# Mixer B's keys turned by VectorE and DMA transfers instead of TensorE, in a fused two-mixer decoder layer on one Trainium2 core

## The chip, the cores and the metric

The kernel runs on one core of a Trainium2 chip. The core has a matrix engine (TensorE, PE in the profile, with its weight loads as PEld), a vector engine (VectorE, DVE), a scalar engine (ScalarE, ACT), GpSimd (POOL), a queue processor (SyncE, SP) that mostly issues transfers, and 16 DMA engines. The metric is device time in microseconds (us), lower is better.

## What is computed

One decoder layer over 512 positions of width 1024. One input projection feeds two token mixers; a gated sum of both goes through an output projection and a layer norm with the residual:

```
h = x @ w_in + b_in
q_a, kv_a, g_nsa, z_a, q_b, f_b, i_b, z_b, gm_a, gm_b = split(h)
o_a = nsa_attention(q_a, kv_a, ...) * silu(z_a)   # 8 heads of 64: compressed, selected, window branch
o_b = hgrn2(q_b, f_b, i_b, lb)                    # 4 heads of 128, chunks of 64
o_b = o_b * rsqrt(mean(o_b^2) + eps) * norm_g * silu(z_b)
y   = sigmoid(gm_a) * (o_a @ w_branch_a) + sigmoid(gm_b) * (o_b @ w_branch_b)
out = layer_norm(alpha * x + y @ w_out)
```

The part that the change touches in mixer B (`hgrn2`) is the state update. Per head, with `k = 1 - f` and `b` the running sum of `log f` in a chunk:

```
kd    = k * exp(b_last - b)
state = dl * state + einsum('bhcd,bhce->bhde', kd, v)
```

The sum runs over positions, so the matrix engine needs `kd` with positions on the partitions; it is made with the key dimension on them. It has to be turned over, for three of the four blocks of 128 positions (the state after the last block is used by nobody).

In mixer A each query tile of 128 positions has softmax probabilities for the selected and the window branch; they too are turned, and then multiplied with the values.

## The kernel before

Everything is fp32 made of two reduced-precision halves: a projection tile is 24 matrix products of 128x512, eight steps of three (high half of the weights by high and low half of x, low half of the weights by the high half). For each weight tile SP loads `wraw`, ScalarE makes the high half (`whi`, L278) and VectorE the low half (`wlo`, L281). Two buffers hold `wraw`, three each `whi` and `wlo`.

The order of the work is written out by a small scheduler in the kernel, the weave. The projection tiles follow each other in a fixed list (queries of B qb0 to qb3, values of B, kcmp, kslc, q1, v0, v1, q0, ..., then the merge gates ga0, gb0, ga1, gb1, ... ga7, gb7, then the branch tiles b0 to b6 and a0 to a6), and every six products the clock of the weave ticks. All other work is generators (`hgrn`, `soften`, `values`, `attn_sum`, `weights`) that yield a number of ticks to wait, taken from a table `D` by `wait_of(step, ...)`. A generator that uses TensorE in a visit of its own first takes a `claim`. Matrix products, transposes and DMA issues are kept in program order on their engines; each engine runs its queue in order, and an instruction that waits holds what stands behind it. TensorE's products all carry the line of one helper, L145, its transposes L149; DMA issues carry L152 (SP), L191 (ScalarE), L194 (GpSimd).

Each projection result is formed in one of two PSUM banks `pa` and evacuated; those of B's values (`proj_i`) by VectorE at L346. The other PSUM banks are pairs as well: `pss`, `pst`, `pso`.

In `hgrn(h)` step h4 turns the keys: `transpose4` runs three 128x128 transposes on TensorE into a `pst` bank, ScalarE copies the 384 columns to SBUF (L472), and four products of 128x128 form the scores of the chunk, which VectorE masks (L478). Step h5 multiplies the turned keys with the values (three products into `pu`), and VectorE adds up the states.

In mixer A, `attn_scores` makes scores for a unit (query tile 3 window, 3 selected, 2, 2, then tile 1 and tile 0 with both branches in one unit); VectorE adds the mask and takes the minimum (L742) straight from `pss`, `pst` and `pso`; `soften` takes exponentials (ScalarE, L759), the sums and gates (L767, L770), scales (L776 on VectorE, L778 on ScalarE), and turns 32x32 blocks with VectorE's transpose into `big` (L792 to L795). Then 16 transfers on SP's queue move the 32-row blocks of `big` to their places in a `turn` buffer. There are two `turn` buffers. `values(u)` then multiplies them with the values in 64-row products into two `pso` banks, in one visit per query tile, and adds the result to `asum` (L836 and L838). `attn_sum` adds the compressed branch.

At the end VectorE finishes the last row tile in three pieces (L1133), each stored as it is made.

Of the kernel before, what the change touches and what calls it, by code (L numbers as in the profile page):

```python
# [9 lines left out]
F32 = mybir.dt.float32  # L10
# [39 lines left out]
def _columns(name):  # L50

    c = np.arange(_COLS[name], _COLS[name] + 128)
    if name[0] == "q" and name[1] != "b" or name[:2] == "za":
# [15 lines left out]

D = dict(h0=6, h2=6, h3=14, h4=0, h5=7, h6=9, n0=20, n1=4, n2=4, n3=0, n4=3, c0=4, c1=5, c2=4, c3=0, r0=5, p0=2,  # L70
         p1=35, p2=1, s0=8, s2=18, s3=4, e0=4, e1=2, t0=6, t1=10, t2=6, t3=3, a4=14, a5=7, y=2, w0=2, w1=1, x0=0,
         x1=0, e2=2, e3=2, g=3, o0=0, o1=9, o2=0, v=10)
D.update({"o0.0": 6, "w0.35": 0, "y.o.3": 6, "o1.1": 3, "h2.0": 4, "y.m.6": 8, "w0.33": 5, "w1.10": 4, "y.m.0": 1,
# [24 lines left out]


def wait_of(step, *at):  # L100
    return D.get(step + "".join(".%s" % a for a in at), D[step])

# [34 lines left out]
def layer_kernel(ctx: ExitStack, tc: tile.TileContext, xT, xn, w0, wi, wf, wv, small, brow, consts,  # L137
# [13 lines left out]
    def dma(o, i):  # L151
        tc.keep_in_program_order(nc.sync.dma_start(o, i))  # L152
# [13 lines left out]
    def T2(n=512, dt=F32):  # L166
        return t2.tile([P, n], dt, name="t2", tag="t2")
# [16 lines left out]
    def PT():  # L184
        return pst.tile([P, 512], F32, name="pst", tag="pst")
# [104 lines left out]
    ident = con[:, K_ID:K_ID + 128]  # L290
# [115 lines left out]

    def transpose4(src, n=4):
        ps = PT()
        for j in range(n):
            T.transpose(ps[:, 128 * j:128 * j + 128], src[:, 128 * j:128 * j + 128], ident)  # L410
        return ps


# [15 lines left out]
    ob = [None] * 4  # L429
    klf, osq, exps, zs = {}, {}, [], {}  # L430
    ngh = cst.tile([P, 4], F32, name="ngh")
    V.tensor_scalar(ngh, sml[:, O_NG:O_NG + 4], 0.5, None, ALU.mult)

    def hgrn(h):
# [22 lines left out]
        A.activation(dlab, cm[:, 1, :, 0], AF.Exp)  # L457
        V.tensor_tensor(e2, e2, k, ALU.mult)
        yield wait_of("h3", h)
        V.tensor_tensor(e1, e1, k, ALU.mult)  # L460
# [8 lines left out]
        yield wait_of("h4", h)  # L469
        kMT = T2()  # L470
        ps = transpose4(e2, 3)
        A.copy(kMT[:, 0:384], ps[:, 0:384])  # L472
        pst_ = PS()
# [6 lines left out]
        yield wait_of("h5", h)  # L480
        while len(vi) < 4:
            yield 1
# [22 lines left out]
        A.activation(sq, o, AF.Square)  # L505
        osq[h] = o, sq

    def hgrn_norm():
# [241 lines left out]
    def soften(visit, scores):  # L750
# [29 lines left out]
        for v, ms, ts, den, parts_ in work:  # L780
# [15 lines left out]
            if ms[-1] == 3:  # L796
                yield wait_of("t3", v)
                while spent[0] < v - 1:
                    yield 1
                w = TURN()  # L800
                to = w.bitcast(F32)[:, 0:1024 * nst].rearrange("p (a x) -> p a x", a=4)
                of = blocks[0][:, 0:1024 * nst].rearrange("p (b x) -> p b x", b=4)
                for a in range(4):
                    for b in range(4):
                        row = 32 * (b ^ 2 * (units[v][1] == (1,)))
                        dma(to[row:row + 32, a], of[32 * a:32 * a + 32, b])
                turned[0] = v + 1
                probs[v] = w.bitcast(F32)[:, 0:1024 * nst].rearrange("p (a c x) -> p c a x", a=4, x=256)
                if units[v][1][-1] == 1:
                    weave.start(values(v), wait_of("t1", v))  # L810

    def values(u):
        i = units[u][0]
        yield from weave.claim(D["t2"])
        tiles = [(v, st) for v in (u - 1, u) if units[v][0] == i for st in range(len(units[v][1]) * (i + 1))]
        accs = PO(), PO()
        todo = []
# [7 lines left out]
        for at, n, half, v, st, br, j, late in sorted(todo):  # L825
            for ab in range(2):
# [3 lines left out]
                         start=n == 0, stop=n == len(tiles) - 1)  # L830
        spent[0] = u + 1
        for half in range(2):
# [47 lines left out]
    qs = []  # L880
    wish = TURN()
    for m in range(4):
# [248 lines left out]
    V.reciprocal(ss[:, 3:4], ss[:, 3:4])  # L1131
    for hf, a, b, store in ((0, 0, 512, dma), (1, 0, 256, dma_act), (1, 256, 512, dma)):
        V.scalar_tensor_tensor(xr[hf][:, a:b], xr[hf][:, a:b], ss[:, 3:4], lbn[hf][:, a:b], ALU.mult, ALU.add)  # L1133
        store(out[384:512, 512 * hf + a:512 * hf + b], xr[hf][:, a:b])
# [79 lines left out]
```

## Time and profile before

| | before |
|---|---|
| time, median of 3 runs | 408.98 us (408.97 to 409.35) |
| profiled execution | 409.05 us, of which span 407.3 us |
| TensorE busy | 399.8 us (98%), 2119 records |
| VectorE busy | 293.6 us (72%) |
| ScalarE busy | 214.6 us (53%) |
| GpSimd busy | 20.8 us (5%) |
| granted TensorE clock | 1.00 of full speed in every stretch shown below |

The span runs from the first to the last instruction of the profiled execution; its time is 1.75 us longer. Matrix products overlap in the pipeline, so one that lasts 0.39 us can follow the one before at a distance of 0.23 us; distances between starts are what counts on TensorE. Idle time on an engine costs something only where TensorE, the one that is nearly always busy, waits for it.

### The profile page before, as it was taken

What the parts mean: (1) busy time and instruction counts of PE and PEld (TensorE: products, weight loads), DVE (VectorE), ACT (ScalarE), POOL (GpSimd) and SP (SyncE); (2) the same over time, 40 slices, a digit from 0 to 9 for tenths busy, and PEclk for the clock granted to TensorE, in tenths of its full rate; (3) what the DMA queues carried; (4) which work ended last, traced back from release to release, by engine and by line L of the source; (5) the groups of instructions that cost most, each with busy time, mean ns of one, the idle gap of its engine ahead of it and who ended that gap; (6) DMA issues with size and microseconds to landing.
All of it is one profiled execution on the core that took longest, in us unless ns stands there. A gap on an engine that the chain in (4) does not pass through costs nothing.

```text
span 407.3 us, 6081 instructions
## 1 busy us (share of the span) xinstructions
PE 399.8 (98%) x2119; PEld 323.8 (80%) x2119; DVE 293.6 (72%) x672; ACT 214.6 (53%) x445; POOL 20.8 (5%) x49
## 2 busy tenths in 40 slices
PE   9999999999999999999999999999999999999993
PEld 8888888899888887778875777867867888888883
DVE  4916599778674978898999777684622969782872
ACT  3445461642224835785688496971316748457201
POOL 2000000001530000004300000000000000000000
PEclk9999999999999999999999999999999999999998
DMA  7975820152333323372273473457958650062121
GB/s 256 378 249 207 276 95 0 32 161 85 117 86 101 123 82 116 104 174 103 64 180 129 155 188 124 106 154 198 265 143 273 206 176 34 0 213 97 52 103 53
DMA packets 26670, 57.62 MB, mean 141 GB/s; under 512 B 5136, under 2 KB 7824, under 8 KB 26640
## 3 DMA queue, kind: packets, MB, share of 16 engines
q1 hardware_dynamic: 25184, 56.69, 44.8%
q8 instruction: 17, 0.28, 0.3%
q10 hardware_dynamic: 432, 0.39, 0.3%
q0 software_dynamic: 1024, 0.15, 0.2%
q14 instruction: 13, 0.11, 0.1%
HBM read 42.12 MB, written 2.10 MB: 109 GB/s over the span
## 4 chain that ended last, share of the span: by engine, by line
PE 90%; DVE 7%; issue 1%; DVEq 0%; ACT 0%; ACTq 0%
PE pa L145 60%; PE pss L145 15%; PE pso L145 11%; PE pst L145 4%; DVE big L792 2%; DVE wlo L281 1%; DVE t L742 1%; DVE t L538 1%; DVE t L544 1%; DVE t L545 0%; PE pst L149 0%; DVE t L537 0%; DVE t L927 0%; DVE big L1133 0%; DVE t L776 0%
## 5 line engine op out<-in xcount | busy, mean ns | idle before, releaser
L145 PE MATMUL pa<-t,whi 128*128 128x512 f32 x640 | 199.9, 394 | 0.0
L145 PEld LDWEIGHTS pa<-t,whi 128*128 128x128 f32 x640 | 118.2, 188 | 28.8 <-issue 4.1
L145 PE MATMUL pa<-t,wlo 128*128 128x512 f32 x320 | 124.9, 390 | 0.1
L281 DVE TENSOR_TENSOR wlo<-wraw,whi 128x1024 fp32r<-128x1024 f32 x44 | 53.5, 1217 | 35.1 <-ACT whi L278 35.1
L278 ACT CAST whi<-wraw 128x1024 fp32r<-128x1024 f32 x44 | 45.7, 1046 | 53.5 <-PE pa L145 35.5
L145 PEld LDWEIGHTS pa<-t,wlo 128*128 128x128 f32 x320 | 60.1, 188 | 13.3 <-DVE wlo L281 0.5
L759 ACT ACTIVATE t<-t,sm_mn 128x512 f32<-128x512 f32 (+3 forms) x64 | 35.2, 552 | 14.9 <-DVE sm_mn L742 14.7
L145 PE MATMUL pso<-t,t 128*128 128x512 f32 (+2 forms) x158 | 33.2, 346 | 0.0
L145 PE MATMUL pss<-t,t 128*128 128x512 f32 (+2 forms) x158 | 30.4, 324 | 0.0
L145 PEld LDWEIGHTS pso<-t,t 128*128 128x128 f32 x158 | 25.8, 195 | 4.1 <-ACT t L237 0.3
L145 PE MATMUL pa<-t,t 128*128 128x512 f32 (+1 forms) x104 | 27.2, 366 | 0.0
L145 PEld LDWEIGHTS pss<-t,t 128*128 128x128 f32 x158 | 23.9, 190 | 2.9
L792 DVE STREAM_TRANSPOSE big<-t 128x512 f32<-128x512 f32 (+3 forms) x48 | 23.5, 523 | 2.2 <-PE pss L145 2.2
L145 PEld LDWEIGHTS pa<-t,t 128*128 128x128 f32 x104 | 18.3, 188 | 3.1
L778 ACT ACTIVATE t<-t,sm_mn 128x128 f32<-128x128 f32 (+3 forms) x42 | 18.6, 512 | 2.5 <-DVE sm_mn L770 2.5
L145 PE MATMUL pa<-turn,t 128*128 128x512 f32 x64 | 19.9, 389 | 0.0
L145 PE MATMUL pss<-t,whi 128*128 128x512 f32 x64 | 19.8, 391 | 0.0
L1007 ACT ACTIVATE t<-pa,hbias 128x512 f32<-128x512 f32 x16 | 10.9, 679 | 12.0 <-PE pa L145 12.0
L205 ACT CAST t<-t 128x512 fp32r<-128x512 f32 x16 | 9.7, 619 | 13.0 <-DVE t L1025 9.5
L145 PE MATMUL pso<-turn,t 64*64 64x512 f32 (+1 forms) x160 | 16.4, 552 | 0.0
L742 DVE CUSTOM_DVE_ANT_0 t<-pss,t 128x128 f32<-128x128 f32 (+3 forms) x24 | 10.2, 476 | 7.4 <-PE pss L145 7.4
L145 PE MATMUL pst<-t,t 128*128 128x512 f32 (+2 forms) x80 | 15.1, 345 | 0.0
(203 smaller groups left out, 531.1 us busy)
## 6 DMA issues: line engine op xcount, KB each, us to landing
wraw<-in_wf_dram SPq DMA_DIRECT2D x38, 512.0 KB, 3.5
turn<-big SPq DMA_DIRECT2D x48, 128.0 KB, 3.6
wraw<-in_wbr_dram SPq DMA_DIRECT2D x8, 512.0 KB, 4.1
t<-in_wout_dram SPq DMA_DIRECT2D x16, 256.0 KB, 4.3
turn<-big SPq DMA_DIRECT2D x32, 96.0 KB, 2.2
t<-in_wi_dram SPq DMA_DIRECT2D x8, 256.0 KB, 5.1
big<-in_w_dram SPq DMA_DIRECT2D x8, 256.0 KB, 7.7
t<-t SPq DMA_DIRECT2D x32, 64.0 KB, 2.0
```

Source lines behind the costliest of these rows:

```text
L145: return tc.keep_in_program_order(nc.tensor.matmul(*a, **k))
L205: A.copy(dst_hi, src)
L278: A.copy(hi, raws[i])
L281: V.tensor_tensor(lo, raws[i], hi.bitcast(F32), ALU.subtract)
L538: V.transpose(rms[h], osq[h][1])
L544: V.tensor_tensor(o, o, rms[h], ALU.mult)
L742: V.tensor_tensor_reduce(out=p[:, c], in0=pg[ab][:, 256 * z:][:, c], in1=amask[:, 512 - n:512], op0=ALU.add, op1=ALU.min, scale=-0.125, sc ...
L759: A.activation(p, p, AF.Exp, bias=mn[:, h:h + 1], scale=-1.0, accum_out=den[:, h:h + 1])
L778: A.mul(p, p, d)
L792: V.transpose(to, of)
L1007: A.activation(gm[name], ps, AF.Tanh, bias=hbias[:, m:m + 1], scale=0.5)
```

## The change

Mixer B's keys no longer go through TensorE. VectorE turns the 32x32 blocks inside the 128x384 tile `e2` in one instruction (into `kT`), and a new generator `turn_keys` moves the blocks to their places in `kMT` by 16 transfers per head, each of 32 rows by 3 pieces of 32 elements, in turn on SP's and on GpSimd's queue. `kT` and `kMT` lie in `keyt`, the second `turn` buffer, which nobody uses at that time. Step h5 waits until all transfers of its head are issued (`keyed`), and their arrival is waited for by the products.

Every turned block of mixer A is moved by 8 transfers on SP and 8 on GpSimd instead of 16 on SP. The values of query tiles 1 and 0 are multiplied in one visit, into `pso` (tile 0) and `pst` banks (tile 1). The last row tile is stored in pieces of 512, 384 and 128 columns instead of 512, 256 and 256. The table `D` of delays has new numbers, so that many instructions stand in another place; of it a few entries are shown.

```diff
-D = dict(h0=6, h2=6, h3=14, h4=0, h5=7, h6=9, n0=20, n1=4, n2=4, n3=0, n4=3, c0=4, c1=5, c2=4, c3=0, r0=5, p0=2,
+D = dict(k0=5, k1=1, h0=6, h2=6, h3=14, h4=0, h5=7, h6=9, n0=20, n1=4, n2=4, n3=0, n4=3, c0=5, c1=5, c2=4, c3=0,
...
-    def transpose4(src, n=4):
-        ps = PT()
-        for j in range(n):
-            T.transpose(ps[:, 128 * j:128 * j + 128], src[:, 128 * j:128 * j + 128], ident)
-        return ps
...
-    klf, osq, exps, zs = {}, {}, [], {}
+    klf, osq, exps, zs, keyed = {}, {}, [], {}, set()
...
         V.tensor_tensor(e2, e2, k, ALU.mult)
+        kT, kMT = (keyt[:, 768 * h + n:768 * h + n + 384] for n in (0, 384))
+        V.transpose(kT, e2[:, 0:384])
+        weave.start(turn_keys(h, kT, kMT), wait_of("k0", h))
         yield wait_of("h3", h)
...
         yield wait_of("h4", h)
-        kMT = T2()
-        ps = transpose4(e2, 3)
-        A.copy(kMT[:, 0:384], ps[:, 0:384])
         pst_ = PS()
...
         yield wait_of("h5", h)
-        while len(vi) < 4:
+        while len(vi) < 4 or h not in keyed:
             yield 1
...
+    def turn_keys(h, src, dst):
+        of, to = (t.rearrange("p (t a x) -> p a t x", t=3, a=4) for t in (src, dst))
+        for a in range(4):
+            for b in range(4):
+                (dma, dma_pool)[b % 2](to[32 * a:32 * a + 32, b], of[32 * b:32 * b + 32, a])
+            yield wait_of("k1", h)
+        keyed.add(h)
...
-                        dma(to[row:row + 32, a], of[32 * a:32 * a + 32, b])
+                        (dma, dma_pool)[b % 2](to[row:row + 32, a], of[32 * a:32 * a + 32, b])
...
-                if units[v][1][-1] == 1:
-                    weave.start(values(v), wait_of("t1", v))
-
-    def values(u):
+                if units[v][1][-1] == 1 and units[v][0] != 1:
+                    weave.start(values(v, *((v - 1,) if units[v][0] == 0 else ())), wait_of("t1", v))
+
+    def values(*done):
+        yield from weave.claim(D["t2"])
+        for u, bank in zip(done, (PO, PT)):
+            products(u, bank(), bank())
+
+    def products(u, *accs):
         i = units[u][0]
-        yield from weave.claim(D["t2"])
...
-        accs = PO(), PO()
...
-    wish = TURN()
+    wish, keyt = TURN(), TURN().bitcast(F32)
...
-    for hf, a, b, store in ((0, 0, 512, dma), (1, 0, 256, dma_act), (1, 256, 512, dma)):
+    for hf, a, b, store in ((0, 0, 512, dma), (1, 0, 384, dma_act), (1, 384, 512, dma)):
```

TensorE, where heads' keys were turned, in the tile q1 (names: `pst<-con,t` is a transpose, `pss<-t,t` the chunk's scores, `pa<-t,whi` and `pa<-t,wlo` the projection). Before:

```order
L145 MATMUL pa<-t_246,whi 128x512
L145 MATMUL pa<-t_247,whi 128x512
L145 MATMUL pa<-t_246,wlo 128x512
L149 MATMUL pst<-con,t_631 128x128 x3
L145 MATMUL pss<-t_661,t_630 128x128 x4
L149 MATMUL pst<-con,t_692 128x128 x3
L145 MATMUL pss<-t_763,t_691 128x128 x4
L145 MATMUL pa<-t_270,whi 128x512
```

And now, in the same tile:

```order
L146 MATMUL pa<-t_197,wlo 128x512
L146 MATMUL pss<-t_653,t_631 128x128 x4
L146 MATMUL pa<-t_222,whi 128x512
L146 MATMUL pa<-t_223,whi 128x512
L146 MATMUL pa<-t_222,wlo 128x512
L146 MATMUL pa<-t_246,whi 128x512
L146 MATMUL pa<-t_247,whi 128x512
L146 MATMUL pa<-t_246,wlo 128x512
L146 MATMUL pss<-t_794,t_705 128x128 x4
L146 MATMUL pa<-t_270,whi 128x512
```

The two sets of scores stand apart and have no transposes ahead of them; of the transposes of `L149` one is left in the whole program (another use, in mixer A).

SP's queue at that time (`wraw` is a weight tile's load, here of v0, v1 and q0; `64x256 x4` moves the rows of the compressed keys, which VectorE adds up right ahead of v1's `wlo`; `32x3x32` are the transfers of the turned keys). Before:

```order
L152 DMA big<-in_w_dram 128x512 x8
L152 DMA wraw<-in_wf_dram 128x1024 x2
L152 DMA t_824<-t_822 64x256 x4
L152 DMA t_855<-in_wv_dram 128x280
L152 DMA t_861<-in_wv_dram 128x280
L152 DMA wraw<-in_wf_dram 128x1024
```

And now:

```order
L153 DMA big<-in_w_dram 128x512 x8
L153 DMA turn<-turn 32x3x32 x10
L153 DMA wraw<-in_wf_dram 128x1024
L153 DMA turn<-turn 32x3x32 x6
L153 DMA wraw<-in_wf_dram 128x1024
L153 DMA turn<-turn 32x3x32 x4
L153 DMA t_875<-t_873 64x256 x4
L153 DMA turn<-turn 32x3x32 x2
L153 DMA t_904<-in_wv_dram 128x280
L153 DMA t_910<-in_wv_dram 128x280
L153 DMA wraw<-in_wf_dram 128x1024
```

Ten transfers stand ahead of the first of these loads, 16 ahead of the second, 20 ahead of the compressed keys' rows.

VectorE around the low half of gb1's weights (`wlo`; `big<-t 128x3x4x32` are transposes of probabilities, `ngh` marks the output of mixer B). Before:

```order
L545 SCALAR_TENSOR_TENSOR t_1481<-t_1481,ngh,t_1585 128x512
L792 STREAM_TRANSPOSE big<-t_1883 128x3x4x32
L792 STREAM_TRANSPOSE big<-t_1885 128x3x4x32
L792 STREAM_TRANSPOSE big<-t_2059 128x3x4x32
L792 STREAM_TRANSPOSE big<-t_2061 128x3x4x32
L792 STREAM_TRANSPOSE big<-t_2063 128x3x4x32
L792 STREAM_TRANSPOSE big<-t_2065 128x3x4x32
L792 STREAM_TRANSPOSE big<-t_2067 128x3x4x32
L792 STREAM_TRANSPOSE big<-t_2069 128x3x4x32
L281 TENSOR_TENSOR wlo<-wraw,whi 128x1024 x2
```

And now:

```order
L541 STREAM_TRANSPOSE t_2313<-t_1521 128x512
L773 TENSOR_TENSOR sm_mn<-sm_mn,gat 128x2 x2
L770 RECIPROCAL sm_mn<-sm_mn 128x2
L547 TENSOR_TENSOR t_1507<-t_1507,t_2286 128x512
L773 TENSOR_TENSOR sm_mn<-sm_mn,gat 128x2
L547 TENSOR_TENSOR t_1328<-t_1328,t_2298 128x512
L282 TENSOR_TENSOR wlo<-wraw,whi 128x1024
L548 SCALAR_TENSOR_TENSOR t_1507<-t_1507,ngh,t_1732 128x512
L548 SCALAR_TENSOR_TENSOR t_1328<-t_1328,ngh,t_2098 128x512
L547 TENSOR_TENSOR t_1520<-t_1520,t_2313 128x512
L795 STREAM_TRANSPOSE big<-t_2104 128x3x4x32
```

Gb1's `wlo` has moved out from behind the eight transposes, and from behind mixer B's last three products with `ngh` (the two instructions of `L281` at the end of the piece before are those of gb1 and ga2).

## Rows read from the trace of the kernel before

**Rows 1.** The page, parts 1 and 2: busy time of each engine, share of the span and instructions; the TensorE clock granted in each of 40 slices of the span, in tenths of full speed.

```profile
PE 399.8 (98%) x2119; PEld 323.8 (80%) x2119; DVE 293.6 (72%) x672; ACT 214.6 (53%) x445; POOL 20.8 (5%) x49
...
PEclk9999999999999999999999999999999999999998
```

**Rows 2.** Four stretches of 20 us: busy us and instructions of PE, PEld, DVE, ACT and POOL, then the granted TensorE clock (1.00 is full speed), the DMA engines' busy share and GB/s.

```profile
60.00:80.00 20.00, 20.00 (x90) 16.57 (x89) 18.24 (x40) 9.13 (x20) 0.26 (x2) 1.00 0.06 20
100.00:120.00 20.00, 20.00 (x119) 17.60 (x117) 12.92 (x25) 6.21 (x10) 9.10 (x18) 1.00 0.33 100
180.00:200.00 20.00, 20.00 (x99) 16.37 (x98) 18.75 (x49) 13.62 (x29) 7.87 (x16) 1.00 0.32 90
220.00:240.00 20.00, 19.91 (x116) 14.02 (x109) 17.01 (x47) 12.91 (x33) 0.00 (x0) 1.00 0.47 142
```

**Rows 3.** The chain that ended last, from 85 to 127 us: start us, us, what. A piece of TensorE on the chain lasts from its start to the start of the next.

```profile
85.46 0.33 PE pst L149 x3
85.79 0.89 PE pss L145 x8
86.68 0.33 PE pst L149 x3
...
100.02 0.33 PE pst L149 x3
...
101.24 0.33 PE pst L149 x3
...
106.73 0.67 PE pss L145 x6
...
113.58 1.34 PE pss L145 x12
...
124.69 1.56 PE pso L145 x14
```

**Rows 4.** TensorE in order of time around the first products of the tile gb1: start us, us, engine, line, operation, count.

```profile
224.16 0.39 PE L145 MATMUL pa<-t,wlo 128*128 128x512 f32 x1
224.39 0.61 PE L145 MATMUL pa<-t,whi 128*128 128x512 f32 x2
225.10 0.50 PE L145 MATMUL pa<-t,wlo 128*128 128x512 f32 x1
225.43 0.62 PE L145 MATMUL pa<-t,whi 128*128 128x512 f32 x2
```

**Rows 5.** The same chain as in Rows 3, from 221 to 226 us.

```profile
221.56 2.37 DVE big L792 x5
223.94 1.12 DVE wlo L281
225.05 0.04 issue
225.10 0.96 PE pa L145 x3
```

**Rows 6.** The same chain again, from 268 to 320 us: the visits for the values of query tiles 2, 1 and 0 (`pso`).

```profile
271.67 4.87 PE pso L145 x44
...
295.82 3.15 PE pso L145 x28
...
314.21 1.45 PE pso L145 x16
```

**Rows 7.** TensorE in order of time around the last of these visits.

```profile
313.82 0.39 PE L145 MATMUL pa<-t,wlo 128*128 128x512 f32 x1
314.14 1.52 PE L145 MATMUL pso<-turn,t 64*64 64x512 f32 x16
315.59 0.73 PE L145 MATMUL pss<-t,whi 128*128 128x512 f32 x2
```

**Rows 8.** A group of instructions of one form on VectorE: line, engine, operation, out<-in, shape, count, busy us, mean ns of one, idle time before.

```profile
L792 DVE STREAM_TRANSPOSE big<-t 128x384 f32<-128x384 f32 x16 | 7.7, 544 | 0.0
```

**Rows 9.** VectorE in order of time from 65 to 70 us (a bracket would name the idle time before an instruction and what ended it).

```profile
65.09 0.69 DVE L346 TENSOR_TENSOR t<-pa,t 128x512 f32<-128x512 f32 x1 [0.86 <-PE pa L145]
65.70 1.22 DVE L437 TENSOR_TENSOR_SCAN t<-t,t 128x512 f32<-128x512 f32 x1
66.84 0.66 DVE L458 TENSOR_TENSOR t<-t,t 128x512 f32<-128x512 f32 x1
...
67.97 1.28 DVE L447 TENSOR_TENSOR t<-sm_cm,t 128x512 f32<-128x512 f32 x2
```

**Rows 10.** TensorE in order of time at three places: the start of the tile kcmp, the tile v1's first product with `wlo`, and the visit for the values of query tile 3.

```profile
70.34 0.61 PE L145 MATMUL pa<-t,whi 128*128 128x512 f32 x2
...
90.40 0.29 PE L145 MATMUL pa<-wlo,t 128*128 128x280 f32 x1
...
214.89 1.52 PE L145 MATMUL pso<-turn,t 64*64 64x512 f32 x12
```

**Rows 11.** Issues of the turned blocks of 128 KB and 96 KB and 64 KB on SP's queue, all 96: ns of one (min/median/max), first and last start.

```profile
L152 SPq DMA_DIRECT2D turn<-big x96: 507/590/2311, 169.3 to 305.2; - x96
```

**Rows 12.** SP's queue in order of time: the four transfers of the compressed keys' rows.

```profile
77.51 2.46 SPq L152 DMA_DIRECT2D t<-t  x4
```

**Rows 13.** GpSimd in order of time: its two sets of 16 transfers.

```profile
107.58 7.95 POOL L194 DMA_DIRECT2D gc<-gq  x16 [1.90 <-DVE gq L619]
...
189.21 7.99 POOL L194 DMA_DIRECT2D t<-t  x16 [52.70 <-DVE t L517]
```

**Rows 14.** VectorE in order of time: the minimum over scores, once while GpSimd issued its second set, and the last one ahead of the visit for query tile 3.

```profile
193.08 0.55 DVE L742 CUSTOM_DVE_ANT_0 t<-pss,t 128x384 f32<-128x384 f32 x1
...
212.06 0.56 DVE L742 CUSTOM_DVE_ANT_0 t<-pso,t 128x384 f32<-128x384 f32 x1
```

**Rows 15.** The page, part 6: transfers by kind, KB each, and the median time in us from issue to landing.

```profile
wraw<-in_wf_dram SPq DMA_DIRECT2D x38, 512.0 KB, 3.5
...
t<-t SPq DMA_DIRECT2D x32, 64.0 KB, 2.0
```

**Rows 16.** The same chain once more, its end.

```profile
397.64 3.13 PE pst L145 x26
...
401.89 0.75 DVE big L1133
...
403.03 0.40 DVE big L1133
```

More of the change, by code (lines that the diff above doesn't have):

```diff
@@ L67 @@
     0, 128, 256, 260, 772, 1284, 1796, 2308, 2820)
-D = dict(h0=6, h2=6, h3=14, h4=0, h5=7, h6=9, n0=20, n1=4, n2=4, n3=0, n4=3, c0=4, c1=5, c2=4, c3=0, r0=5, p0=2,
-         p1=35, p2=1, s0=8, s2=18, s3=4, e0=4, e1=2, t0=6, t1=10, t2=6, t3=3, a4=14, a5=7, y=2, w0=2, w1=1, x0=0,
-         x1=0, e2=2, e3=2, g=3, o0=0, o1=9, o2=0, v=10)
-D.update({"o0.0": 6, "w0.35": 0, "y.o.3": 6, "o1.1": 3, "h2.0": 4, "y.m.6": 8, "w0.33": 5, "w1.10": 4, "y.m.0": 1,
[7 rows of a table removed]
+D = dict(k0=5, k1=1, h0=6, h2=6, h3=14, h4=0, h5=7, h6=9, n0=20, n1=4, n2=4, n3=0, n4=3, c0=5, c1=5, c2=4, c3=0,
+         r0=5, p0=2, p1=35, p2=1, s0=4, s2=18, s3=4, e0=4, e1=2, t0=6, t1=10, t2=6, t3=2, a4=22, a5=5, y=2, w0=2,
+         w1=1, x0=0, x1=0, e2=2, e3=2, g=3, o0=0, o1=9, o2=0, v=10)
+D.update({"o0.0": 6, "w0.35": 0, "y.o.3": 7, "o1.1": 3, "h2.0": 3, "y.m.6": 8, "w0.33": 5, "w1.10": 4, "y.m.0": 1,
[7 rows of a table added]
           "w0.42": 7, "y.za0": 12, "y.m.4": 3, "w0.7": 3, "w0.25": 0, "y.m.2": 0, "y.o.5": 5, "w0.3": 4, "o1.7": 10,
           "y.p.1": 5, "x1.a.5": 4, "w0.19": 0, "w0.14": 0, "x0.gb3": 4, "x1.b.1": 5, "w1.41": 0, "o2.3": 4,
[2 rows of a table removed]
[2 rows of a table added]
           "x1.b.4": 5, "e1.1.2": 1, "x0.zb0": 1, "x0.za3": 1, "e3.3.0": 4, "t0.3.2": 7, "g.0.2": 7, "w0.21": 1,
@@ L830, in values @@
                          start=n == 0, stop=n == len(tiles) - 1)
-        spent[0] = u + 1
+        spent[0] = max(spent[0], u + 1)
         for half in range(2):
```

35 rows, old and new, of tables (w1, x1) are left out of this document.

## The prediction

> **What bounds the kernel now.** I read the busy shares first, then the stretches, then the chain of waits, and then each place of the change in order of time on the engine concerned. TensorE is busy 399.8 of 407.3 us, at a clock granted at 1.00 of full speed, its upper level of 2.4 GHz [rows 1]. In the stretches of 20 us that matter it is busy for all 20.00, but for one with 19.91 [rows 2]. So the chain runs along TensorE, and what counts is how much TensorE has to issue. Work that leaves TensorE is a gain of its full length, as long as nothing that TensorE reads comes late in its place; work on VectorE, ScalarE and the queues costs nothing until then. VectorE is the engine to watch: 18.24, 18.75 and 17.01 us busy of 20 in three of the stretches.
>
> The one place where TensorE waits for late data is the tile gb1. Its first two products with `whi` start at 224.39, the regular distance to the next one would put it at 224.39 + 2 x 0.23 = 224.85, and it starts at 225.10; the one behind follows after 0.33 instead of 0.23. That is 0.25 + 0.10, with roundings 0.36 us [rows 4]. The chain says why: eight transposes of probabilities stood on VectorE ahead of gb1's `wlo`, which was made from 223.94 to 225.05 [rows 5].
>
> **The change part by part.** All terms are against the profiled execution, 409.05 us; the median of the runs is 0.07 below it.
>
> *Twelve transposes leave TensorE.* On the chain they are four pieces of 0.33 us [rows 3]: 4 x 0.33 = 1.32 us. They stood in one visit with the chunk's scores, and now two visits become more. That costs nothing that the rows can show: six records of 128x128 took 0.67 and twelve 1.34 [rows 3], 0.112 each, with no fixed part. Term: -1.32.
>
> *What takes their place on VectorE.* Four 32x32-block transposes of 128x384, 544 ns each [rows 8], so 4 x 0.54 = 2.2 us (1.9 if they overlap as neighbours there do), in a stretch with 20 - 18.24 = 1.76 us left [rows 2]. ScalarE loses four copies, which it had time for. This is not hidden by idle time alone but by slack. The tightest place is the evacuation of B's values: the tile kcmp, at 70.34 [rows 10], needs the `pa` bank of the third of these tiles, and its evacuation began at 65.09 and ended at 65.78 [rows 9]. Behind the second evacuation, which I put at 61.0 to 61.6, the new order has two scans, four differences, two products, one transpose and small ones ahead of the third: 2 x 1.14 + 4 x 0.6 + 2 x 0.58 + 0.46, some 0.9 of small ones and 0.6 for the second evacuation itself [rows 8, 9], 7.8 us in all, so the third ends at 69.2 to 69.8. Cover left: 0.5 to 1.1 us. Term: 0; if the cover goes, what is late comes off the gain.
>
> *The transfers of the turned keys.* SP issues 32 of them, GpSimd 32. The trace has none of 3 pieces per row. SP's issues of turned blocks took 507 ns at least, 590 in the middle, 2311 at most with their waits [rows 11], and the small ones 2.46/4 = 0.62 [rows 12]; I take 0.62 and keep 0.5 to 2.3. On SP, 16 stand ahead of v1's load and 20 ahead of the rows of the compressed keys, and on VectorE v1's `wlo` stands behind the sums that read these rows. From VectorE's first transpose at about 61, with c per issue: 61.4 + 20c + 0.7 for two loads + 2.46 for the rows + 2.0 to land [rows 12, 15] + about 3 for the sums and `wlo`, 69.6 + 20c. TensorE reads it at 90.40 [rows 10], some 0.65 us earlier now, when two of the four pieces are gone. At c = 0.62 it is there at 82; the cover ends at c = (89.75 - 69.6)/20 = 1.0 us. GpSimd's 32 were 0.50 us each in both sets that the trace has (7.95/16 and 7.99/16, [rows 13]); from 61 they end about 77. The last head's products follow the visit of 124.69 to 126.25 [rows 3], about 125 now: cover until (125 - 61)/32 = 2.0 us per issue. Term: 0.
>
> Whether VectorE's work holds back GpSimd's issues is shown by two rows: 0.50 us each with VectorE at 12.92 of 20 and at 18.75 of 20 [rows 2, 13], and an instruction of VectorE inside the second set took 0.55, outside it 0.56 [rows 14]. The Trainium skill, "SBUF — State Buffer", section "SBUF: two separate sides", states the opposite risk: certain VectorE instructions lock GpSimd out of a shared port, and a transfer issued from GpSimd that takes about 620 ns alone took about 3100 beside such a one. By that rule, if it met every issue, the last transfer would leave at an estimated 61 + 32 x 3.1 = 160 us and TensorE would wait some 35 us. The trace speaks against it.
>
> *gb1's wait.* The new order puts gb1's `wlo` ahead of six of the eight transposes and of three scalings and a product. From the last minimum over scores, which ended at 212.62 [rows 14], 11.3 us passed before it; now three transposes of 128x512, two of 128x384, two products and small ones stand between, about 5 us, so it ends near 219, five us before it is read. The wait of 0.36 goes. What is late next: the same stretch of VectorE up to that minimum holds by the durations of the same forms about 1.5 us more work and 0.8 less idle time, less what starts earlier; TensorE's visit for query tile 3, which reuses the banks that the minimum reads, stands at 214.89 [rows 10] and comes at about 213.6. Cover: 1.0 to 1.6 us instead of 2.3. Term: -0.36.
>
> *One visit for tiles 1 and 0.* Their two visits take 3.15 + 1.45 us on the chain [rows 6]. Going into a visit of 64-row products costs 0.32 - 0.23 = 0.09 us and leaving 0.73 - 0.62 = 0.11 more than the regular distance [rows 7]. One entry and exit less is -0.20. Against it, tile 2's visit, with as many products but more wide ones, took 4.87, 0.27 more than both together [rows 6]: at that rate +0.07. I take -0.1, halfway, and keep -0.2 to +0.07.
>
> *Turned blocks on two queues.* SP spends half the time on each block, so its weight loads stand less long behind them; TensorE waited for none of them, so 0. *The last stores.* The chain ends with 3.13 us of TensorE, then VectorE's pieces [rows 16]; three pieces of the same sum of columns, one store larger and the last smaller: 0, with 0.15 on either side.
>
> Sum: 409.05 - 1.32 - 0.36 - 0.1 = 407.27, less nothing for the median: **407.3 us**, 0.4% below 408.98. A difference of under 0.2%, 0.8 us, can't be told from no change here.
>
> **The rivals.**
> A, slower: SP's issue with 3 pieces per row is dear. It decides from 1.0 us; each 0.1 us above costs 20 x 0.1 = 2 us of TensorE's waiting in the tile v1. At 1.2 us: 407.3 + 4 = 411.3. For it: three times the runs per transfer, and rows up to 2.3 us. Against: the median of 0.59 is over transfers of very different sizes.
> B, slower: GpSimd's issues are held by VectorE's busy stretch, past 2.0 us each. At 2.2 the last head's products wait 32 x 0.2 = 6.4 us: 413.7. Against: both sets at 0.50.
> C, VectorE is late: the third evacuation at kcmp or the minimum ahead of tile 3 overruns its cover of about one us, and 0.5 to 1.5 us come back: 407.8 to 408.8, say 408.4. For it: the loads of [rows 2]. Against: the covers as counted.
> D, the wait at gb1 only moves to another tile's `wlo`: 407.3 + 0.4 = 407.7. For it: VectorE has no less to do. Against: `wlo` now stands earlier.
> That the transposes are still there is excluded by the order of the new program.
>
> **How the numbers follow.** Forecast 0.64, its own range 406.9 to 407.6 (the bounds of the merged visit, the stores, and 0.1 of scatter); D 0.12, C 0.12, A 0.08, B 0.04. Faster by over 0.2% means below 408.16: forecast, D and about a fifth of C, 0.78 less 0.01 for mishaps without a name, 0.77. Within 0.2%: the rest of C and a part of B that waits little, 0.11. Slower: A, most of B, 0.12. The range takes the forecast from 406.8 and reaches over D and most of C to 408.8, which leaves out A and B and a little at both ends.
>
> **What would show it.** TensorE's transposes of 128x128 fall from 13 to one. The products of gb1 stand at 0.23 us throughout, and the chain has no `wlo` ahead of them. TensorE at kcmp, at v1's first `wlo` and at tile 3's visit shows no distance above the regular. SP's issues of keys stay below 1.0 us, GpSimd's below 2.0, both near 0.6 and 0.5. One of these over its bound, with a TensorE start delayed behind it, makes the forecast wrong; a time under 406.8 would mean that TensorE had a cost around the transposes that I do not see.

## The result, and the profile after

The changed kernel took **406.19 us**, median of 4 runs (405.98 to 406.42), against 409.08 for the kernel before beside it (408.97 to 409.35): ratio 0.993, 95% interval 0.9918 to 0.9942. The forecast was 407.3, the range 406.8 to 408.8; the time lies below both. The same kernel, repeated later, gave 407.02 over 6 runs (406.29 to 408.44, ratio 0.9956, 0.994 to 0.9972). The median of all ten is 406.46. The wider spread of the repeat has a cause of its own, below.

The page of the profiled execution (405.98 us, span 404.2), parts 1 and 4, against [rows 1]: busy time, share and instructions of each engine, then the chain's shares by engine.

```profile
PE 397.3 (98%) x2107; PEld 322.4 (80%) x2107; DVE 294.2 (73%) x676; ACT 212.9 (53%) x441; POOL 61.0 (15%) x129
...
PE 98%; DVE 0%; DVEq 0%; issue 0%; ACT 0%; ACTq 0%
```

TensorE has twelve records fewer and VectorE four more; GpSimd's 80 more are the transfers it now issues. Up to TensorE's last product the chain is TensorE alone, where before VectorE's `wlo` stood in it [rows 5].

Next, three of the stretches of [rows 2], with the same columns.

```profile
60.00:80.00 20.00, 20.00 (x90) 16.57 (x89) 19.27 (x42) 8.76 (x19) 16.06 (x32) 1.00 0.37 93
...
180.00:200.00 20.00, 20.00 (x99) 16.37 (x98) 20.00 (x47) 15.24 (x29) 9.73 (x20) 1.00 0.23 70
220.00:240.00 20.00, 20.00 (x97) 16.07 (x96) 15.12 (x44) 13.80 (x35) 3.94 (x8) 1.00 0.56 158
```

VectorE is at 19.27 and 20.00 of 20 us, and TensorE is busy throughout at the full granted clock, now from 220 to 240 us too, where it had 19.91. At gb1, where [rows 4] showed 0.71 and 0.33 between starts, TensorE in order of time reads:

```profile
222.57 0.61 PE L146 MATMUL pa<-t,whi 128*128 128x512 f32 x2
223.02 0.39 PE L146 MATMUL pa<-t,wlo 128*128 128x512 f32 x1
223.25 0.61 PE L146 MATMUL pa<-t,whi 128*128 128x512 f32 x2
```

0.45 for two products and 0.23 for one: the wait is gone. VectorE made that `wlo` long before:

```profile
215.07 1.22 DVE L282 TENSOR_TENSOR wlo<-wraw,whi 128x1024 fp32r<-128x1024 f32 x1
```

The issues of the keys (`turn<-turn`) and of the probabilities (`turn<-big`), by queue: ns of one (min/median/max), first and last start.

```profile
L153 SPq DMA_DIRECT2D turn<-turn x32: 585/598/1074, 60.8 to 90.9; - x32
L153 SPq DMA_DIRECT2D turn<-big x48: 507/592/2644, 167.5 to 298.6; - x48
L195 POOL DMA_DIRECT2D turn<-turn x32: 545/545/691, 61.1 to 81.1; - x32
L195 POOL DMA_DIRECT2D turn<-big x48: 489/496/531, 165.6 to 293.9; - x48
```

Three pieces per row cost 0.598 us on SP and 0.545 on GpSimd, close to the 0.62 and 0.50 that the prediction reckoned with and below the 1.0 and 2.0 from which it would have been decided. The first key transfers of GpSimd ran beside VectorE at 19.27 of 20 us; the longest issue took 0.691 us. The Trainium skill, "SBUF — State Buffer", section "SBUF: two separate sides", says that certain VectorE instructions lock GpSimd out, and gives some 3100 ns for a transfer beside such a one. None of GpSimd's 80 issues of blocks in this run comes near that; whether any of VectorE's instructions beside them was of the locking kind, no run here shows.

**Where the time came from.** I measured the distance between the same projection products in the two traces, so that only what TensorE does between them counts. Transposes -1.33; waits at gb0 and gb1 -0.05 and -0.36; the visits for tiles 1 and 0 -0.37; from TensorE's end to the span's end 6.51 to 6.06, -0.45. That is -2.56.

The two profiled executions are 3.07 apart. Of the 0.5 left, 0.38 is there before the first product of the first projection tile, at 26.82 us in before and 26.44 in after. Most of it lies in the first twelve products of 128x256: behind the first of them, in before five follow at 0.19 to 0.21 us and the rest at 0.12, in after one at 0.18 and the rest at 0.11 to 0.13. The product behind these twelve starts anywhere between 5.80 and 6.53 us in 14 profiles of whatever kernel (before 6.26, after 5.94), so no edit is credited with it: in this pair the changed kernel was lucky. Another 0.06 lies in the products right behind the visit, and the rest in small steps.

409.05 - 2.56 = 406.49. The ten runs have 406.46, but at least one of them holds a wait that is explained below, so that the closeness is partly chance; the version without that wait (`a_h3_pool`, below) took 406.40.

### The profile page after: what moved, and what is told of

Read it like the earlier page. It is cut to its first block, busy times and chain, and to the rows that moved or that the text cites. A ratio compares the mean times of both kernels' runs of the same rounds, so it can differ in the third digit from the quotient of the medians.

```text
span 404.2 us, 6238 instructions
## 1 busy us (share of the span) xinstructions
PE 397.3 (98%) x2107; PEld 322.4 (80%) x2107; DVE 294.2 (73%) x676; ACT 212.9 (53%) x441; POOL 61.0 (15%) x129
## 4 chain that ended last, share of the span: by engine, by line
PE 98%; DVE 0%; DVEq 0%; issue 0%; ACT 0%; ACTq 0%
PE pa L146 66%; PE pss L146 15%; PE pso L146 12%; PE pst L146 5%; DVE big L1139 0%; DVEq L1216 0%; DVE big L1136 0%; ACT t L1134 0%; PE pst L150 0%; DVE sm_ss L1137 0%; ACTq L1134 0%
## 5 line engine op out<-in xcount | busy, mean ns | idle before, releaser
L195 POOL DMA_DIRECT2D turn<-big x48 | 23.4, 496 | 120.7 <-DVE kcB L605 43.4
L762 ACT ACTIVATE t<-t,sm_mn 128x512 f32<-128x512 f32 (+3 forms) x64 | 35.2, 553 | 11.3 <-DVE sm_mn L745 11.1
L146 PE MATMUL pss<-t,t 128*128 128x512 f32 (+2 forms) x134 | 27.2, 333 | 0.0
L195 POOL DMA_DIRECT2D turn<-turn x32 | 17.5, 551 | 61.3 <-DVE turn L455 60.4
L146 PEld LDWEIGHTS pss<-t,t 128*128 128x128 f32 x134 | 21.0, 190 | 2.8
L146 PEld LDWEIGHTS pst<-t,t 128*128 128x128 f32 x80 | 13.0, 189 | 1.9
```

The costliest lines, as they stand in the source:

```text
L146: return tc.keep_in_program_order(nc.tensor.matmul(*a, **k))
L195: tc.keep_in_program_order(G.dma_start(o, i))
L762: A.activation(p, p, AF.Exp, bias=mn[:, h:h + 1], scale=-1.0, accum_out=den[:, h:h + 1])
```

## The experiments

Each time is a median with its range; the kernel before gave 409.03 or 409.06 beside them. "After" is the changed kernel. The interval behind a ratio is at 95%.

**Are the transposes worth their length?** After with the keys on TensorE again:

```diff
-        V.transpose(kT, e2[:, 0:384])
-        weave.start(turn_keys(h, kT, kMT), wait_of("k0", h))
...
+        ps = PT()
+        for j in range(3):
+            T.transpose(ps[:, 128 * j:128 * j + 128], e2[:, 128 * j:128 * j + 128], ident)
+        A.copy(kMT[:, 0:384], ps[:, 0:384])
...
```

> The changed kernel with the keys turned by TensorE again (12 transposes, 4 copies on ScalarE, no transfers of keys). Theory 1: the transposes are worth their own length, 12 x 0.11 = 1.33, so 407.5, if nothing else on TensorE changes. Rival (taking them away saved more than their length, and with it what the prediction missed): 408.3 to 409. Rival (VectorE, relieved, or the queues move something else): a wait on TensorE that the trace shows.

407.42 us (407.29 to 408.17), ratio 0.9964 (0.9952 to 0.9976). Its chain has the four pieces back, of which the first is

```profile
83.88 0.33 PE pst L150 x3
84.21 0.89 PE pss L146 x8
```

and against after the distances grow by 0.335, 0.331, 0.333 and 0.330 there, 1.33 together; the rest of TensorE's time between the first and the last product grows by 0.11, in steps of 0.04 at most. So -1.32 was right. The medians show less, 1.02 against `a_h3_pool`, the version that has no wait at 100 us either, with the start as uncertain as said above.

**Is the merged visit worth 0.1 or more?** After with two visits:

```diff
-                if units[v][1][-1] == 1 and units[v][0] != 1:
-                    weave.start(values(v, *((v - 1,) if units[v][0] == 0 else ())), wait_of("t1", v))
+                if units[v][1][-1] == 1:
+                    weave.start(values(v), wait_of("t1", v))
```

> The changed kernel with the values of query tiles 1 and 0 in two visits again. Theory 1: a visit of 64-row products costs 0.09 on entry and 0.05 more on its first group, 0.12 behind its last group and 0.11 on the first product after it, 0.37 in all, so 406.19 + 0.37 = 406.56 and the products of the two visits take 5.03 us instead of 4.66. The prediction's step (0.1 to 0.2): 406.3 to 406.4.

408.56 (406.41 to 410.72), ratio 0.9987 (0.997 to 1.0004): far too scattered. Its trace has the 0.44 of the visits, and a wait of TensorE at 100 us that has nothing to do with them. The same edit on the version without that wait (`a_h3_pool`, below), where it can be read:

> The version without the wait at 100 us (last head's keys on GpSimd's queue, 406.40), with the values of query tiles 1 and 0 in two visits again. Theory 1: +0.37 to +0.44, 406.8, and the span of these products grows by that on TensorE. The prediction's step: +0.1 (at most 0.2), 406.5 to 406.6.

406.93 (406.64 to 409.04), ratio 0.9949 (0.9931 to 0.9968), against 406.40: +0.53 by the medians, whose intervals overlap, and +0.43 on TensorE by the traces, which is what the reading rests on. Its chain, to be held against [rows 6]:

```profile
289.80 4.08 PE pa L146 x18
293.88 3.16 PE pso L146 x28
297.03 15.24 PE pa L146 x66
...
313.63 1.45 PE pso L146 x16
315.08 1.58 PE pss L146 x6
```

and that of after, with one visit:

```profile
289.78 18.81 PE pa L146 x83
...
309.95 1.45 PE pso L146 x16
311.40 2.99 PE pst L146 x28
314.40 1.60 PE pss L146 x6
```

The visits take 1.45 + 2.99 = 4.44 instead of 3.16 + 1.45 = 4.61, which is 0.17. The 66 projection products behind the first visit take 15.24, where 18.81 / 83 x 66 = 14.96 is regular: another 0.28. With 0.02 back in `pss`, 0.43.

The pieces of the chain don't say where in a visit this lies. TensorE in order of time around the first of the two visits does:

```profile
293.49 0.39 PE L146 MATMUL pa<-t,wlo 128*128 128x512 f32 x1
293.81 3.24 PE L146 MATMUL pso<-turn,t 64*64 64x512 f32 x32
296.97 0.74 PE L146 MATMUL pa<-t,whi 128*128 128x512 f32 x2
297.56 0.40 PE L146 MATMUL pa<-t,wlo 128*128 128x512 f32 x1
```

By the exact starts the entry takes 0.319 instead of 0.227, the first group of four products 0.460 instead of 0.409, the step behind the last group 0.318 instead of 0.193, the product behind that 0.342 instead of 0.227, and those that follow are some 0.06 longer together. So the 0.2 that I had counted outside the visit is there; what I had not counted, another 0.2, is mostly inside.

**Does the store's size move the end?** After with stores of 256 and 256 columns, and before with 384 and 128:

```diff
-    for hf, a, b, store in ((0, 0, 512, dma), (1, 0, 384, dma_act), (1, 384, 512, dma)):
+    for hf, a, b, store in ((0, 0, 512, dma), (1, 0, 256, dma_act), (1, 256, 512, dma)):
```

> The changed kernel with the last stores back at 512, 256 and 256 columns, nothing else. Between the last product's end and the span's end the changed kernel took 0.49 us less than before; the two traces put 0.09 of it at the last store (from issue to the wait's end 2.01 instead of 2.10) and 0.35 at GpSimd's last instructions (0.08 instead of 0.43 us between its last drain and its final semaphores). Theory 1 (small store, GpSimd's end is its own matter): 406.19 + 0.1 = 406.3, and the gap on GpSimd stays at 0.08. Rival (the smaller last store is worth all 0.49): 406.7.

> The kernel before with only the last stores changed to 512, 384 and 128 columns. Theory 1: 409.08 - 0.1 = 409.0, with the gap of 0.43 us on GpSimd still there. Rival (the store is worth 0.49): 408.6.

407.54 (406.04 to 410.19), ratio 0.9969 (0.9952 to 0.9986), and 409.18 (408.51 to 411.07), ratio 1.0006 (0.9995 to 1.0016). The second says that the store is worth nothing that can be measured: from its issue to the end of SP's wait for it pass 2.07 us instead of 2.10. The first is blurred by the same wait at 100 us, 0.82 in its profile; its end behind TensorE is 6.10, that of after 6.06. So the store can account for less than 0.1 of the 0.45 at the end.

**What do the two queues for the turned blocks do?** Before with that edit alone:

```diff
-                        dma(to[row:row + 32, a], of[32 * a:32 * a + 32, b])
+                        (dma, dma_pool)[b % 2](to[row:row + 32, a], of[32 * a:32 * a + 32, b])
```

> The kernel before with only the turned blocks of mixer A on two queues. Prediction's step: 0 on TensorE's path, 409.06. Theory 1 on GpSimd's end: the gap between GpSimd's last drain and its final semaphores was 0.40 us in both kernels with the old GpSimd program (49 instructions) and 0.045 in four with longer ones; with 89 instructions it goes, and the time is 408.7. Rival (the gap goes with something else in the change): 0.40 again, 409.06.

408.36 (407.81 to 408.8), ratio 0.9983 (0.9974 to 0.9992): 0.67 by the medians, where I had put 0. Two things in its trace. gb1's products on TensorE, with the old table of numbers:

```profile
224.43 0.62 PE L145 MATMUL pa<-t,whi 128*128 128x512 f32 x2
224.88 0.39 PE L145 MATMUL pa<-t,wlo 128*128 128x512 f32 x1
```

No wait: with the blocks on two queues `wlo` comes ahead of six of the eight transposes in VectorE's order, and at gb0 and gb1 together TensorE waits 0.42 less. And the end: GpSimd's last instructions. The last line of the program on GpSimd's queue, first of before, then of after: ns of one, first and last start.

```profile
L1210 POOLq EVENT_SEMAPHORE  x4: 17/17/17, 406.2 to 407.2; - x4
L1210 POOLq DRAIN  x3: 34/102/2862, 196.2 to 406.6; - x3
```

```profile
L1216 POOLq EVENT_SEMAPHORE  x4: 17/17/17, 403.5 to 404.1; - x4
L1216 POOLq DRAIN  x3: 34/102/6454, 293.9 to 403.9; - x3
```

By these rounded times 0.6 us pass from the last drain to the last semaphore in before and 0.2 in after; by the exact times of the trace, from the drain's end to the first semaphore behind it, 0.40 and 0.045. It is 0.40 in both kernels where GpSimd issues none of the turned blocks (before, and before with the other stores), and 0.044 in before with two queues. To see whether it is the transfers or just the length of GpSimd's program, before with 40 tiny fills on GpSimd at the start, every other engine's order as it was:

```diff
+    for _ in range(40):
+        G.memset(epst, EPS)
```

> The kernel before with 40 more fills of one small tile on GpSimd at the very start, every other engine's order unchanged. Theory 1 (the 0.40 us between GpSimd's last drain and its last semaphores depend on how its program ends, by its length alone): the gap falls to 0.045 and the time to 408.7. Rival (it needs the transfers on GpSimd's queue, or it is the run's own chance): 0.40, 409.05.

408.55 (408.19 to 410.52), ratio 0.9988 (0.9976 to 1.0001). Its rows of the same view:

```profile
L1212 POOLq EVENT_SEMAPHORE  x4: 17/17/17, 406.3 to 407.0; - x4
L1212 POOLq DRAIN  x3: 34/102/2895, 196.3 to 406.8; - x3
```

0.2 between them, 0.044 by the exact times: a longer program on GpSimd ends 0.35 sooner behind its drain, with fills as with transfers. The median is 0.5 lower, in an interval that just reaches no change; in the profile the stretch from TensorE's end to the span's end is 0.36 shorter. Only this one length of fills was tried, and why it matters is not shown.

**Why did after scatter?** The repeat, unedited, beside two variants that put the last head's keys all on GpSimd, or all on SP:

```diff
-                (dma, dma_pool)[b % 2](to[32 * a:32 * a + 32, b], of[32 * b:32 * b + 32, a])
+                (dma, dma_pool)[b % 2 or h == 3](to[32 * a:32 * a + 32, b], of[32 * b:32 * b + 32, a])
```

```diff
+                (dma, dma_pool)[b % 2 and h < 3](to[32 * a:32 * a + 32, b], of[32 * b:32 * b + 32, a])
```

> The changed kernel, nothing edited. Two kernels that issue the same products on TensorE up to 290 us spread from 406.0 to 410.7 over their runs, and in their profiles TensorE waited 0.8 and 1.5 us at 100 us for a pa bank: VectorE's evacuation of v's first tile (L386) stood behind two sums (L656, L657) that waited for transfers t<-t, which SP issued behind the keys' transfers. Theory 2 (that wait belongs to the change and comes and goes with the landing of these transfers): the changed kernel spreads too, from 406.0 to above 408, with a median of 406.2 to 407.5. Rival (it belongs to the edits of those two kernels or to that chip alone): 406.0 to 406.5 as in the first four runs.

> The changed kernel with the last head's (h 3) 16 key transfers all on GpSimd's queue, so 8 issues (4.8 us) less on SP ahead of the transfers t<-t. Theory 2: these land 3 to 5 us earlier, the wait at 100 us never comes, 406.0 to 406.4 with no spread beyond that of the kernel before. Rival (GpSimd's queue is the slow one, or VectorE's own lateness makes the wait): spread and median as in the changed kernel.

> The suspected cost doubled: the last head's 16 key transfers all on SP's queue, 8 issues (4.8 us) more ahead of t<-t. Theory 2: TensorE waits some 4 us at 100 us in every run, 410 to 411.5. Rival (SP's queue is not what delays them): as the changed kernel.

407.02 (406.29 to 408.44); 406.40 (406.02 to 406.69), ratio 0.9934 (0.9922 to 0.9946); 414.28 (413.81 to 415.45), ratio 1.0133 (1.0118 to 1.0147). The repeat's chain of waits around 98 us:

```profile
94.00 0.59 SPq L153
...
94.63 3.54 DMA t<-t
...
98.29 0.70 DVE t L656
99.02 0.69 DVE t L657
99.71 0.37 DVE t L386
...
100.12 1.80 PE pa L146 x12
```

Read it from below. TensorE needs a `pa` bank; VectorE evacuates it at L386; ahead of that, in order, VectorE stands on L656 and L657, which read four rope rows `t<-t`; SP issues these behind the keys. In before the same four left SP at 90.04, in the first profile of after at 92.22, in the repeat at 92.76:

```profile
89.46 2.57 SPq L153 DMA_DIRECT2D turn<-turn  x4
...
92.76 2.46 SPq L153 DMA_DIRECT2D t<-t  x4
```

In the first profile the evacuation ends at 97.80 + 0.44 = 98.24 and TensorE's next product with `whi` starts at 98.77: a cover of 0.53 us. In the repeat the last of the rows took 3.54 us to land, and the same step on TensorE, 0.58 in the first profile, takes 100.12 - 98.28 = 1.84: a wait of 1.26.

```profile
98.28 0.83 PE L146 MATMUL pss<-t,turn 128*128 128x128 f32 x6
100.12 0.40 PE L146 MATMUL pa<-whi,t 128*128 128x280 f32 x1 [1.02 <-DVE t L386]
```

With the last head's keys on GpSimd the rows leave SP at 90.06 as in before, the evacuation starts at 96.84, TensorE doesn't wait, and the scatter shrinks from 2.15 to 0.67 us in five runs. (It is not the only scatter: one run in seven of `h_two_visits`, which has the same order, took 409.04.) With them on SP eight keys stand ahead and the rows leave at 97.77; TensorE starts at 105.39, 4.4 us late, after 1.6 a little earlier. That makes 6.1 of the 9.5 us between the two profiled executions (415.45 and 405.98). Most of the rest is in its stretches (columns as in [rows 2]):

```profile
100.00:105.30 5.30, 1.20 (x11) 1.01 (x9) 1.71 (x4) 0.24 (x1) 0.00 (x0) 0.95 0.56 174
105.30:111.60 6.30, 6.21 (x27) 6.21 (x28) 4.35 (x10) 1.43 (x2) 0.41 (x2) 0.50 0.12 21
111.60:120.00 8.40, 8.40 (x44) 7.16 (x43) 4.06 (x9) 2.85 (x4) 2.79 (x7) 1.00 0.41 134
```

After a stretch with 1.20 us of work in 5.30 the granted clock is 0.50, the level of 1.2 GHz, for 6.3 us: products of 128x280 come every 0.23 us instead of 0.13, and some 2.8 us more are lost.

**Do the two queues still matter in the new arrangement?** `a_h3_pool` with the turned blocks all on SP:

```diff
-                        (dma, dma_pool)[b % 2](to[row:row + 32, a], of[32 * a:32 * a + 32, b])
+                        dma(to[row:row + 32, a], of[32 * a:32 * a + 32, b])
```

> The same version with the turned blocks of mixer A all on SP's queue again. Theory 1: VectorE's instructions then stand as before the change, gb1's wlo behind eight transposes, and TensorE's waits at gb0 and gb1 are back, +0.4: 406.8; the end on GpSimd stays short (it still has 97 instructions). Rival (the new table of delays took the waits away, as the prediction has it): 406.4.

409.06 (408.62 to 412.36), ratio 1.0015 (0.9997 to 1.0033): 2.66 slower than with two queues, several times what I expected. The waits at gb0 and gb1 are back with 0.4, and a new one of 1.6 us stands at 236 us. The chain leads back to a late weight load and from there to gb1's `wlo`:

```profile
222.34 1.12 DVE wlo L282
223.46 0.02 issue
223.48 4.71 DMA wraw<-in_wf_dram
...
234.17 3.28 ACT t L762 x12
237.45 0.58 ACT t L1013
...
238.08 3.92 PE pa L146 x16
```

The load leaves 0.02 us behind the `wlo`, which reads one of the two `wraw` buffers and in this run stands behind all eight transposes again. So by this chain both waits go back to VectorE's order and not to what stands ahead of the load on SP's queue. Further on, twelve instructions of the softmax (L762) stand on ScalarE ahead of its evacuation L1013; in before, where the `wlo` is as late, that evacuation comes ahead of them and TensorE doesn't wait at this place.

**A version with one visit less.** `a_h3_pool` with the sum over branches (`attn_sum`) moved right behind the last scores, without a visit of its own:

```diff
-        yield from weave.claim(3)
-        pc = [PS(), PS(), PT(), PT()]
+        pc = [PO(), PO(), PT(), PT()]
```

and 32 for 22 at `a4`.

> The version without the wait at 100 us, with one more visit of 64-row products joined to another: the compressed branch's products (attn_sum) right behind the last scores, in pso and pst banks, without a claim of their own. Theory 1 (each such visit costs some 0.3 to 0.4 us at its edges): 406.0 to 406.1. Rival (a bank or VectorE makes it wait): 406.4 or more, with a wait at 262 us.

406.05 (405.73 to 406.65), ratio 0.9922 (0.9906 to 0.9938): 0.35 below `a_h3_pool` by the medians, 0.23 on TensorE by the traces. It is the lowest median of all, but its interval overlaps those of `a_h3_pool` and of the changed kernel, so by the times alone it is not shown to be faster than these.

## Why the prediction was wrong

The direction and the main term were right, the size was short: -1.78 forecast, -2.56 measured term by term. Two terms failed. The end of the program, put at 0 under *The last stores*, measured -0.45; the merged visit, put at -0.1, measured -0.37 to -0.43. The prediction's own reading of a time under 406.8, a cost around the transposes that it didn't see, was wrong as well: putting the transposes back costs their own length, 1.33.

Luck had a part on both sides. The pair of the first profiles holds some 0.4 of the start that belongs to no edit. And the repeat's 407.02 lies inside the range with a wait that the prediction had not seen, 1.26 us in its profile, which hides part of the gain. Step by step:

- *Twelve transposes leave TensorE*, -1.32: -1.33 by trace, and back when they are put back.
- *What takes their place on VectorE*, 0: the third evacuation ahead of kcmp ended at 69.03 (predicted 69.2 to 69.8) and kcmp started at 69.96. v1's `wlo` ended at 84.39 (predicted 82) and was read at 89.37. The last minimum ended at 210.80, 2.3 us ahead of the visit at 213.07: the cover that the prediction saw shrink to 1.0 to 1.6 stayed as it was. Rival C didn't come, at these places.
- *gb1's wait*, -0.36: -0.41 with gb0's 0.05. The size holds, and so does the order of VectorE's work that was read; what makes that order was not seen. I gave it to the new order of the weave and booked the two queues at 0; the kernel before with only two queues loses the wait as well, and `a_h3_pool` with one queue gets it back. Rival D didn't come.
- *One visit for tiles 1 and 0*, -0.1: this term was mis-sized. It measured -0.37 to -0.43, outside its own bounds of -0.2 to +0.07. From the rows I took the 0.2 outside a visit and halved it, by tile 2's rate. But a visit costs inside as well: its first group of four took 0.460 and not the 0.409 of the others, and behind the last group 0.12 more pass. 0.09 + 0.05 + 0.12 + 0.11 = 0.37, and some 0.06 in the products that follow.
- *The last stores*, 0 with 0.15 on either side: -0.45, of which 0.35 is the end of GpSimd's program and 0.03 to 0.09 the store. I looked at the end of the chain and not at what each engine does behind it. VectorE's pieces did come out even: 2.68 and 2.67 us from TensorE's end to theirs.
- *Turned blocks on two queues*, 0, "TensorE waited for none of them": alone they are worth 0.67 in before, and undoing them costs 2.66. The 0.67 is no further gain: its trace has 0.42 less at gb0 and gb1 and 0.36 less at GpSimd's end (and a start 0.1 later), which are in the terms above. TensorE did wait for what these transfers decide: they changed the order in which VectorE's work was laid out, and with it the time of gb1's `wlo` and of the load that needs its buffer.
- *The transfers of the turned keys*, 0: the price per issue was right, 0.598 for 0.62. But I followed SP's queue to two readers, v1 and the compressed rows, and left out a third, the rope rows. Rival A's mechanism is real, and it decides not at 1.0 us per issue but at the normal 0.6, at another place: 0, 0.8, 1.3 and 1.5 us in the four profiles with that order on SP's queue. This error goes the other way and hid part of the gain. Rival B, GpSimd held back, didn't come.

## What to carry to other kernels

When transfers move onto a queue, list every load behind them and follow each to the instruction that reads it and to what stands behind that in order on its engine; a PSUM bank evacuated behind a waiting instruction counts too. A cover of half a microsecond can show as scatter and not in the first runs, so repeat the kernel before comparing variants of it. Undo each part alone: here an edit booked at nothing was worth 0.67 us by itself, half of the one that the change is named for.

## What the runs showed that I had not expected

- A visit of 64-row products among 128-row ones cost 0.37 us in edges, two of the four parts inside it, and some 0.06 in the 128-row products that followed.
- GpSimd's last semaphores came 0.40 us behind its drain with a short program, 0.044 with 40 fills or 48 transfers more. The reason stays open.
- The last of the four transfers of rope rows took 2.43, 3.54, 3.81 and 3.99 us to land in four profiles (`a_store256`, `a_again`, `a_h3_sp`, `a_two_visits`); why it varies stays open too.
- One wait of 4.4 us cost TensorE some 2.8 us more through the clock, granted at 0.50 for 6.3 us behind it.
